# Loading and scaling a layer's residual 512 columns at a time within its output projection, in a two-layer decoder trunk

## The chip, the cores and the metric

The kernel runs on one core of one Trainium2 chip. The metric is the device time of one execution in microseconds (us), median of several runs. The engines are PE (TensorE: matmuls and transposes), DVE (VectorE), ACT (ScalarE), POOL (GpSimd) and SP (SyncE, which here issues transfers only). SP and POOL each have a DMA queue from which they issue transfers in program order. On-chip data lies in SBUF, 128 partitions wide; matmuls write PSUM, eight banks here, of which the kernel uses four for projections (`pjb`) and four for the rest (`mxb`).

## The reference

Two layers over 256 tokens of 2048 columns, all in float32: layer 0 mixes the tokens by a gated linear recurrence, layer 1 by a sparse attention. Each ends with an output projection, a residual and a layer norm:

```python
D_MODEL, SEQ, DEPTH = 2048, 256, 2
DEEPNORM_ALPHA = (2 * DEPTH) ** 0.25
def _layer_norm(x, g, b):
    mu = jnp.mean(x, -1, keepdims=True)
    xc = x - mu
    var = jnp.mean(xc * xc, -1, keepdims=True)
    return xc * lax.rsqrt(var + LN_EPS) * g + b
h = x
for i in range(DEPTH):
    y = _hgrn2_mixer(h, ...) if i == 0 else _nsa_mixer(h, ...)   # ends with (o * silu(z)) @ w_out
    h = _layer_norm(DEEPNORM_ALPHA * h + y, ln_g, ln_b)
```

For layer 1, `h` in `ALPHA * h` is the output of layer 0's norm, that is its normalized rows times `l0_ln_g` plus `l0_ln_b`. Applying these two to the normalized rows is the work that the change moves.

## The kernel before

The two tiles (`NT = 2`) of 128 tokens each are worked on through a list of projections with a weight matrix. Weights come in pieces of 256 rows by 512 columns (512 KB), loaded by `load` (L105) from SP's queue into a few slots named `wr`. So that one-pass products carry float32, each piece is split into a high part `wh` (ACT, L78) and a low part `wl` (DVE, L79), and the activations likewise (`bh` and `bl` for the input of layer 1's output projection, `ah` and `al` before). `tok_step` makes three matmuls for each tile and each 128 rows: high by high (L140), high by the weights' low (L141), low by high (L142). A piece of the output projection is 12 matmuls of 512 columns.

Layer 1's attention has four head groups: `query(g)` projects the queries (L185 to L188 and their kin), then `scores` makes the probabilities `p` (maximum, exponentials on ACT at L729 and L732, sums, L734 to L737 for the factors, L746 for the scaling of `p` on DVE), and `values` transposes `p` on PE (L762) and multiplies by the values, with a last copy on ACT (L774). `gate(g)` then multiplies by a gate (`zT`, ACT L786; DVE L789). Groups 2 and 3 are queried first and gated behind; so the last stretch of attention holds the scores and values of group 3 and the gate projections of groups 2 and 3, and PE's order there mixes the first pieces of the output projection among them.

The output projection of layer 1 has four column blocks `c` of 512 columns, each of 8 pieces. Blocks 0 to 2 go through `project`, block 3 through `project_by_tile`. Behind each block, `residual` adds `ALPHA * xr` to the product on DVE (L831) into `hb`, and takes the statistics (L833); behind the last block the norm follows and the output is stored (L854).

The residual itself: layer 0 leaves its normalized rows, before gain and bias, in a DRAM tile `norm0`. Behind the attention's code stands a loop over the four column blocks. It loads 512 columns of `norm0` for both tiles into `xr` (512 KB, L804), the gain and the bias of these columns, each broadcast to 128 partitions, into `gb` (256 KB each, L807), all from POOL's queue, and on POOL multiplies (L809) and adds (L810) for each tile. `xr` and `gb` take the slots of layer 1's multiplied input (`ah`, `al`), which are free after its last gate projection has read them. The pool `n1` with `hb` comes to be where attention's buffers were. The rows `l1_ln_g` and `l1_ln_b` of the last norm (1 MB each) are loaded by `row` (L820) from SP's queue, behind block 1 in the code.

The order of each engine's instructions isn't that of the code. `tile.TileContext(nc, schedule_with_timeline_sim=True)` orders them by a simulated timeline, data dependences, buffers and priorities; `parts` raises the priority of the weight splits. The engines then run their lists in order and wait for each other by semaphores.

Of the kernel before, what the change touches and what calls it, by code (L numbers as in the profile page):

```python
# [17 lines left out]
D = 2048  # L18
# [11 lines left out]
# the compressed blocks in the order that the kernel has them  # L30
# [5 lines left out]
# 500000 ** (-arange(0, 32, 2) / 32) in float32  # L36
# [5 lines left out]
# 2 pi in parts whose products with a small integer are exact  # L42
# [4 lines left out]
# The pairs of tokens in the order that the kernel has them: the second tile's are reversed.  # L47
PAIRS = list(range(64)) + list(range(127, 63, -1))
# column of each segment of l1_w_in
# [5 lines left out]
def trunk(ctx, tc, a, out):  # L55
# [20 lines left out]
    def split(hi, lo, src):  # L76
        """src = hi + lo, exactly, each of which the single pass products carry."""
        act.activation(hi, src, AF.Copy)  # L78
        dve.tensor_tensor(lo, src, hi.bitcast(F32), op=OP.subtract)  # L79

# [7 lines left out]
    class Pair:  # L88
        """Transposed activations, split: KG pairs of [128, 4, S]."""
# [12 lines left out]
    def load(w, j, c0, n):  # L102
        """Rows 256j .. 256j+255 of columns c0 .. c0+n-1."""
        raw = slot([128, 2, n], F32, "wr", 3, 1)
        nc.sync.dma_start(raw, w[256 * j:256 * (j + 1), c0:c0 + n].rearrange("(k p) n -> p k n", p=128))  # L105
        return raw
# [4 lines left out]
    # While there is room, a second pool holds a part of the slots.  # L111
# [13 lines left out]
    def slot(shape, dtype, name, n, more):  # L125
        """A tile of the n slots of a name, or of the n + more while there is room."""
# [17 lines left out]
    def project(xs, w, c0, also=None, n=512):  # L144
        """[tokens, n columns] of xs @ w, a bank for each tile of tokens."""
# [10 lines left out]
    def project_by_tile(xs, w, c0, after, behind=None, halve=False):  # L156
        """The same, one tile of tokens after the other, with after(t, bank) behind each. If that
        (or behind, for the first tile) names a matmul, the rest of the next tile's are queued after it."""
        ws = [weights(w, j, c0, 512) for j in range(KT // 2)]
        for t in range(NT):  # L160
            # the last one in two halves, where that is asked for
# [11 lines left out]
    def project_t(xs, w, c0, before=None):  # L173
        """[512 columns, tokens] of xs @ w: a bank for each two blocks of 128 columns."""
        ps = [pjb([128, 2, S]) for _ in range(2)]
        for j in range(KT // 2):
            hi, lo = before(j) if before else weights(w, j, c0, 512)
            for kk in range(2):
                k = 2 * j + kk
                xh, xl = xs.at(k, slice(0, S))  # L180
                for b in range(4):
                    o = ps[b // 2][:, b % 2]
                    c = slice(128 * b, 128 * (b + 1))
                    # one clearing of the bank serves both of its blocks
# [7 lines left out]
    def transposed(src):  # L192
        """[128 tokens, 4, 128] -> a bank of [128, 4, 128 tokens]."""
# [12 lines left out]
    # own[s, t]: s is t  # L206
    own = masks0.tile([128, 128], I32, name="own")
    # first[s, b]: s is the first of the b-th pair
    first = masks0.tile([128, 64], I32, name="first")
    # lvl[s, i, t, (b, j)]: s lies in the earlier half (the second one, in the second tile of tokens)  # L210
    # of the b-th block of 2m, m = 2 << i
    lvl = masks0.tile([128, 6, NT, 64], I32, name="lvl")
    # additive masks of the scores
# [12 lines left out]
    def columns(p, src):  # L226
        """A row of D values as a bank's [128, KT]."""
# [6 lines left out]
    def masks(p):  # L234
# [16 lines left out]
        # lower bounds of the forget gates: the softmax over one layer, less its first row  # L251
# [9 lines left out]
    def tables(p):  # L261
        dve.tensor_copy(g0c, columns(p, a["l0_ln_g"].rearrange("(k d) -> k d", d=128)))
        dve.tensor_copy(b0c, columns(p, a["l0_ln_b"].rearrange("(k d) -> k d", d=128)))
        # the tokens by partition and by column, and the last token of each compressed block
# [18 lines left out]
        # rotary tables  # L283
# [25 lines left out]
    w0 = a["l0_w_in"]  # L309

    # x, transposed, just ahead of the first projection's need of it
    xT = Pair("a")
    with tc.tile_pool(name="start", bufs=4) as start:
        # keeps the tensor engine's clock up until the first operands are there
# [37 lines left out]
    def recurrence(g, m0, ad, pf, pq):  # L352
        """The decayed scores of four heads, keys by queries: within a tile of tokens (into ad), and
        the first tile's keys with the second tile's queries. Built by doubling, with products of
        forget gates only, none of which exceeds one."""
# [14 lines left out]
        # within a pair of tokens: the products of each token's own query and key, and of the later  # L370
        # one's query with the earlier one's key, added up over the partitions
# [25 lines left out]
        for i in range(7):  # L397
# [10 lines left out]
            else:  # L408
                # The first tile's earlier halves and the second's, whose blocks are reversed, are
                # complementary: they are the keys of both tiles' later halves at once.  # L410
# [82 lines left out]
    def moments(p, hb, stats, t):  # L493
        """Mean and 1 / deviation of a row, from its chunks' statistics."""
# [42 lines left out]
    # Four blocks of 64 keys are what the top four select, and no key is further than the window:  # L537
    # both attend to every earlier key.
# [5 lines left out]
    def three(o, a, b, start, stop):  # L544
        """o += a @ b, of split operands."""
# [4 lines left out]
    def rotary(p, t, ps):  # L550
        """Out of the bank, and the first 32 of each head rotated."""
# [11 lines left out]
    class Compression:  # L563
        """The blocks of 32 keys or values, every 16 tokens, through the two layers of their MLP."""
# [4 lines left out]
        def flatten(self, src):  # L569
            """src: [128, 4, S] -> [d, place in the block, group, block], split."""  # L570
# [9 lines left out]
            # chunks of 16 tokens, in which the second tile's pairs are in reverse  # L580
            c = src.rearrange("p g (c l) -> p l g c", l=16)
            for i in range(2):
                fl = self.p.tile([128, 16, 4, NB], F32, name="fl")
                # (places among the blocks, the chunk of the first of them)
# [11 lines left out]
        def step(self, i):  # L596
            """The i-th eighth of the first layer."""
# [203 lines left out]
    for c in range(4):  # L801
# [4 lines left out]
        for i, name in enumerate(("l0_ln_g", "l0_ln_b")):  # L806
            nc.gpsimd.dma_start(gb[:, i], a[name][None, cs].to_broadcast([128, 512]))  # L807
# [90 lines left out]
```

## Time and profile before

| what | value |
|---|---|
| median of 3 runs | 1029.81 us |
| the three runs | 1028.95, 1029.81, 1035.2 us |
| span of the profiled execution | 1024.8 us |
| median of the runs less that span | 5.0 us |
| PE busy | 1000.4 us, 98% of the span |
| DVE, ACT, POOL busy | 66%, 53%, 14% |
| moved by DMA | 185.25 MB, 181 GB/s |

The profiled execution's own time is known as its span, from the first to the last instruction that the profiler recorded; the 5.0 us between it and the median lie around the span. Busy shares are of the span. Matmuls are pipelined, so that the duration of one overlaps that of the next: the pace is read from starts, not from durations.

### The profile page before, as it was taken

The numbers are of one execution on the slowest core, as the hardware profiler recorded it, in microseconds if no ns is written. First come the engines' busy times: TensorE is split into PE (matmuls) and PEld (weight loads), VectorE is DVE, ScalarE is ACT, GpSimd is POOL, SyncE is SP. The second block draws the span as 40 slices with busy tenths as digits, with TensorE's granted clock in tenths as the row PEclk, the third lists the DMA queues.
The fourth block names the chain that finished last, engine by engine and source line by source line (L and its number), as shares of the span: only waits on it lengthen the run. The fifth ranks groups of instructions, "written<-read, shape, count | busy, mean of one in ns | idle before, by whom it ended". The sixth has DMA issues, their size and how long they took to land.

```text
span 1024.8 us, 15936 instructions
## 1 busy us (share of the span) xinstructions
PE 1000.4 (98%) x6041; PEld 883.5 (86%) x6041; DVE 680.9 (66%) x1095; ACT 543.5 (53%) x864; POOL 148.5 (14%) x234
## 2 busy tenths in 40 slices
PE   9999999999999999999999999999999999979995
PEld 8988998899889988878889777989889889967885
DVE  6796568656865686656555566556857667885666
ACT  6654445444544454433575455455748666764431
POOL 0400300030003000310016310101020021180003
PEclk9999999999999999999999999999999999998998
DMA  8765465555555554457555677575453555564752
GB/s 293 259 219 164 155 185 165 165 157 183 164 165 160 183 163 164 165 192 248 174 192 171 202 236 232 149 231 180 144 149 119 154 156 155 164 215 149 262 164 82
DMA packets 99756, 185.25 MB, mean 181 GB/s; under 512 B 6096, under 2 KB 20512, under 8 KB 99168
## 3 DMA queue, kind: packets, MB, share of 16 engines
q1 hardware_dynamic: 96992, 174.48, 53.4%
q0 software_dynamic: 2688, 9.76, 3.2%
q8 instruction: 47, 0.77, 0.3%
q14 instruction: 29, 0.24, 0.1%
HBM read 180.02 MB, written 4.19 MB: 180 GB/s over the span
## 4 chain that ended last, share of the span: by engine, by line
PE 89%; DVE 4%; DMA 3%; ACT 2%; POOL 1%; issue 1%; SPq 0%; ACTq 0%; DVEq 0%
PE pjb L141 17%; PE pjb L142 17%; PE pjb L140 17%; PE pjb L185 9%; PE pjb L187 9%; PE pjb L188 9%; PE mxb L423 2%; DMA wr<-in_l_w_in_dram 1%; POOL fl L590 1%; PE mxb L196 1%; DVE wl L79 1%; PE mxb L546 1%; ACT wh L78 1%; PE mxb L547 1%; PE mxb L548 1%; PE mxb L762 1%
## 5 line engine op out<-in xcount | busy, mean ns | idle before, releaser
L79 DVE TENSOR_TENSOR wl<-wr,wh 128x1024 fp32r<-128x1024 f32 (+2 forms) x330 | 397.6, 1209 | 218.6 <-ACT wh L78 215.5
L78 ACT ACTIVATE wh<-wr 128x1024 fp32r<-128x1024 f32 (+2 forms) x330 | 340.3, 1036 | 334.6 <-PE pjb L142 150.8
L185 PE MATMUL pjb<-ah,wh 128*128 128x256 f32 x832 | 235.4, 284 | 0.7 <-ACT wh L78 0.7
L187 PE MATMUL pjb<-al,wh 128*128 128x256 f32 x832 | 235.4, 284 | 0.0
L188 PE MATMUL pjb<-ah,wl 128*128 128x256 f32 x832 | 234.3, 283 | 0.5 <-DVE wl L79 0.5
L141 PE MATMUL pjb<-wl,ah 128*128 128x512 f32 (+1 forms) x576 | 223.0, 387 | 2.5 <-DVE wl L79 2.4
L142 PE MATMUL pjb<-wh,al 128*128 128x512 f32 (+1 forms) x576 | 222.0, 386 | 0.0
L140 PE MATMUL pjb<-wh,ah 128*128 128x512 f32 (+1 forms) x576 | 221.0, 387 | 0.8 <-ACT wh L78 0.6
L185 PEld LDWEIGHTS pjb<-ah,wh 128*128 128x128 f32 x832 | 156.8, 189 | 1.7 <-ACT wh L78 1.1
L188 PEld LDWEIGHTS pjb<-ah,wl 128*128 128x128 f32 x832 | 156.2, 189 | 1.4 <-DVE wl L79 1.3
L187 PEld LDWEIGHTS pjb<-al,wh 128*128 128x128 f32 x832 | 156.1, 188 | 0.5
L141 PEld LDWEIGHTS pjb<-wl,ah 128*128 128x128 f32 x576 | 108.5, 188 | 26.6 <-DVE wl L79 5.2
L140 PEld LDWEIGHTS pjb<-wh,ah 128*128 128x128 f32 x576 | 108.0, 188 | 23.2 <-ACT wh L78 1.7
L142 PEld LDWEIGHTS pjb<-wh,al 128*128 128x128 f32 x576 | 108.5, 188 | 22.0
L141 PE MATMUL pjb<-wl,bh 128*128 128x512 f32 (+1 forms) x272 | 105.4, 387 | 0.0
L142 PE MATMUL pjb<-wh,bl 128*128 128x512 f32 (+1 forms) x272 | 105.0, 386 | 0.0
L140 PE MATMUL pjb<-wh,bh 128*128 128x512 f32 (+1 forms) x272 | 104.9, 386 | 0.0
L142 PEld LDWEIGHTS pjb<-wh,bl 128*128 128x128 f32 x272 | 51.8, 190 | 11.0 <-issue 0.2
L141 PEld LDWEIGHTS pjb<-wl,bh 128*128 128x128 f32 x272 | 51.8, 190 | 10.9
L140 PEld LDWEIGHTS pjb<-wh,bh 128*128 128x128 f32 x272 | 51.6, 190 | 10.9
L486 POOL TENSOR_TENSOR gz<-gz,gn 128x512 f32<-128x512 f32 x8 | 13.5, 1692 | 316.1 <-ACT gz L485 315.5
L557 POOL TENSOR_TENSOR rot<-qr,cc 128x128 f32<-128x128 f32 x14 | 9.5, 678 | 252.4 <-ACT qr L553 252.0
(223 smaller groups left out, 1054.0 us busy)
## 6 DMA issues: line engine op xcount, KB each, us to landing
wr<-in_l_w_in_dram SPq DMA_DIRECT2D x230, 512.0 KB, 3.6
wr<-in_l_w_out_dram SPq DMA_DIRECT2D x64, 512.0 KB, 4.3
wr<-in_l_w_in_dram SPq DMA_DIRECT2D x16, 280.0 KB, 2.9
wr<-in_l_cmp_w_k_dram SPq DMA_DIRECT2D x8, 512.0 KB, 4.1
wr<-in_l_cmp_w_v_dram SPq DMA_DIRECT2D x8, 512.0 KB, 4.2
xr<-in_x_dram POOLq DMA_DIRECT2D x4, 512.0 KB, 5.3
norm<-hb POOLq DMA_DIRECT2D x2, 1024.0 KB, 5.5
xr<-norm POOLq DMA_DIRECT2D x4, 512.0 KB, 6.8
```

What stands on the lines that cost most here:

```text
L78: act.activation(hi, src, AF.Copy)
L79: dve.tensor_tensor(lo, src, hi.bitcast(F32), op=OP.subtract)
L140: pe.matmul(ps, xh, wh, start=(k == 0), stop=False)
L141: pe.matmul(ps, xh, wl, start=False, stop=False)
L142: pe.matmul(ps, xl, wh, start=False, stop=(k == KT - 1))
L185: pe.matmul(o, hi[:, kk, c], xh, start=(k == 0 and b % 2 == 0), stop=False, skip_group_check=True)
L187: pe.matmul(o, hi[:, kk, c], xl, start=False, stop=False, skip_group_check=True)
L188: pe.matmul(o, lo[:, kk, c], xh, start=False, stop=(k == KT - 1), skip_group_check=True)
L196: last[0] = pe.transpose(ps[:, i], src[:, i], ident).ins
L423: pe.matmul(ps[:, h], km[:, h].rearrange("p b r j -> p (b r j)"), later, start=True, stop=True)
L486: pool.tensor_tensor(z, z, gn, op=OP.mult)
L546: pe.matmul(o, a[0], b[0], start=start, stop=False)
```

## The change

The loop behind attention goes. `fetch(c)` does the same for one block: it loads `xr` and `gb` from SP's queue, the weights' own, and multiplies and adds on POOL. It is called within the projection of its block: `project` gets a function `behind`, which it calls behind each piece's matmuls, and which fetches at the fourth piece (`j == 3`); the fetch of block 3 stands behind block 2. `xr` and `gb` now lie in the pool `n1`, `xr` in two buffers, `gb` in one. The diff, without lines in which only comments went:

```diff
@@ behind gate(3, os3)
-    # the residual of layer 1, in the slots of the activations that have been multiplied
-    xs = []
-    for c in range(4):
-        cs = slice(512 * c, 512 * (c + 1))
-        xr = acts.tile([128, NT, 512], F32, name="xr", tag="ah")
-        nc.gpsimd.dma_start(xr, norm0[:, cs].rearrange("(t p) d -> p t d", p=128))
-        gb = acts.tile([128, 2, 512], F32, name="gb", tag="al")
-        for i, name in enumerate(("l0_ln_g", "l0_ln_b")):
-            nc.gpsimd.dma_start(gb[:, i], a[name][None, cs].to_broadcast([128, 512]))
-        for t in range(NT):
-            pool.tensor_tensor(xr[:, t], xr[:, t], gb[:, 0], op=OP.mult)
-            pool.tensor_tensor(xr[:, t], xr[:, t], gb[:, 1], op=OP.add)
-        xs.append(xr)
...
+    def fetch(c):
+        cs = slice(512 * c, 512 * (c + 1))
+        xr = n1.tile([128, NT, 512], F32, name="xr")
+        nc.sync.dma_start(xr, norm0[:, cs].rearrange("(t p) d -> p t d", p=128))
+        gb = n1.tile([128, 2, 512], F32, name="gb", bufs=1)
+        for i, name in enumerate(("l0_ln_g", "l0_ln_b")):
+            nc.sync.dma_start(gb[:, i], a[name][None, cs].to_broadcast([128, 512]))
+        for t in range(NT):
+            pool.tensor_tensor(xr[:, t], xr[:, t], gb[:, 0], op=OP.mult)
+            pool.tensor_tensor(xr[:, t], xr[:, t], gb[:, 1], op=OP.add)
+        return xr
...
     for c in range(4):
         cs = slice(512 * c, 512 * (c + 1))
-        def residual(t, ps, c=c, xr=xs[c], parts=range(2)):
+        xr = []
+
+        def behind(j, c=c, xr=xr):
+            if j == 3:
+                xr.append(fetch(c))
+
+        def residual(t, ps, c=c, xr=xr, parts=range(2)):
+            xr = xr[0]
...
         if c < 3:
-            for t, ps in enumerate(project(oT, a["l1_w_out"], 512 * c)):
+            for t, ps in enumerate(project(oT, a["l1_w_out"], 512 * c, behind)):
                 residual(t, ps)
+            if c == 2:
+                last_xr = fetch(3)
             if c == 1:
                 widen()
                 g1, b1 = row("l1_ln_g"), row("l1_ln_b")
         else:
+            xr.append(last_xr)
             project_by_tile(oT, a["l1_w_out"], 512 * c, finish, halve=True)
```

SP's queue in the output projection, before; L105 loads a weight piece, L820 the rows of the last norm, L854 stores the output:

```order
L105 DMA wr<-in_l_w_out_dram 128x2x512 x15
L820 DMA l_ln_g<-in_l_ln_g_dram 128x2048
L820 DMA l_ln_b<-in_l_ln_b_dram 128x2048
L105 DMA wr<-in_l_w_out_dram 128x2x512 x17
L854 DMA out_dram<-hb 128x512 x8
```

And in the changed kernel, where L808 loads `xr`, L811 gain and bias, L819 the rows of the last norm:

```order
L105 DMA wr<-in_l_w_out_dram 128x2x512 x15
L808 DMA xr<-norm_72 128x2x512
L811 DMA gb<-in_l_ln_g_dram 128x512
L811 DMA gb<-in_l_ln_b_dram 128x512
L808 DMA xr<-norm_72 128x2x512
L819 DMA l_ln_g<-in_l_ln_g_dram 128x2048
L819 DMA l_ln_b<-in_l_ln_b_dram 128x2048
L105 DMA wr<-in_l_w_out_dram 128x2x512 x3
L811 DMA gb<-in_l_ln_g_dram 128x512
L811 DMA gb<-in_l_ln_b_dram 128x512
L808 DMA xr<-norm_72 128x2x512
L105 DMA wr<-in_l_w_out_dram 128x2x512 x3
```

The four residual loads and the eight of gain and bias stand among the pieces now; ahead of the piece numbered 14 (one of the 15 before it is a later piece, 19, which has a slot of its own) stand `xr` and `gb` of block 0 and `xr` of block 1 beside the two rows that stood there before.

DVE's order behind the last gate, before; `bl` is the low part of the projection's input, `wl` that of a piece, L831 the residual addition, L833 the statistics:

```order
L79 TENSOR_TENSOR bl<-o,bh 128x4x128 x2
L79 TENSOR_TENSOR wl<-wr,wh 128x1024 x3
L831 SCALAR_TENSOR_TENSOR hb<-xr,pjb 128x256 x2
L833 BN_STATS stats<-hb 128x6
L831 SCALAR_TENSOR_TENSOR hb<-xr,pjb 128x256 x2
L833 BN_STATS stats<-hb 128x6 x3
L79 TENSOR_TENSOR wl<-wr,wh 128x1024 x6
L831 SCALAR_TENSOR_TENSOR hb<-xr,pjb 128x256 x2
```

And in the changed kernel, where L837 is the residual addition and L839 the statistics:

```order
L79 TENSOR_TENSOR bl<-o,bh 128x4x128 x2
L79 TENSOR_TENSOR wl<-wr,wh 128x1024 x3
L837 SCALAR_TENSOR_TENSOR hb<-xr,pjb 128x256 x2
L839 BN_STATS stats<-hb 128x6 x2
L837 SCALAR_TENSOR_TENSOR hb<-xr,pjb 128x256 x2
L839 BN_STATS stats<-hb 128x6 x2
L79 TENSOR_TENSOR wl<-wr,wh 128x1024 x3
L837 SCALAR_TENSOR_TENSOR hb<-xr,pjb 128x256 x2
L839 BN_STATS stats<-hb 128x6 x2
L79 TENSOR_TENSOR wl<-wr,wh 128x1024
```

The residual addition of block 0 stands in the same place, ahead of the splits of pieces 14 to 16; that of block 1 stands three splits further up than before, ahead of pieces 17 to 19. On PE, ACT and DVE nothing ahead of these rows is ordered otherwise.

## Rows read from the trace of the kernel before

**Rows 1.** The page's head: busy us, share of the span and instructions.

```profile
PE 1000.4 (98%) x6041; PEld 883.5 (86%) x6041; DVE 680.9 (66%) x1095; ACT 543.5 (53%) x864; POOL 148.5 (14%) x234
```

**Rows 2.** Windows: stretch, us, busy (instructions) per engine, granted clock, DMA share, GB/s.

```profile
914.60:924.40 9.80, 2.33 (x9) 1.13 (x8) 7.98 (x9) 4.83 (x13) 9.50 (x8) 0.74 0.32 123
924.40:929.60 5.20, 5.16 (x15) 4.14 (x16) 4.68 (x7) 2.04 (x3) 0.00 (x0) 0.51 0.38 125
```

**Rows 3.** PE's timeline: start us, us, line, operation, out<-in.

```profile
914.24 0.39 PE L140 MATMUL pjb<-wh,bh 128*128 128x512 f32 x1
917.36 0.40 PE L142 MATMUL pjb<-wh,bl 128*128 128x512 f32 x1
929.80 0.39 PE L140 MATMUL pjb<-wh,bh 128*128 128x512 f32 x1
963.20 0.40 PE L141 MATMUL pjb<-wl,bh 128*128 128x512 f32 x1
971.64 0.39 PE L141 MATMUL pjb<-wl,bh 128*128 128x512 f32 x1
```

**Rows 4.** PE's groups, 914.7 to 929.75: busy us, mean ns, idle before, releasers.

```profile
L762 PE MATMUL mxb<-ident,p 128*128 128x128 f32 x8 | 2.5, 411 | 7.5 <-DVE p L746 5.3 <-ACT o L774 2.2
```

**Rows 5.** The chain of waits, 903 to 925: start us, us, what.

```profile
904.03 7.17 DMA wr<-in_l_w_out_dram
911.29 1.06 ACT wh L78
912.36 1.28 ACT L729
916.35 1.01 DVE st L734
922.90 1.49 DVE p L746
```

**Rows 6.** Landing of L105's loads, 880 to 1000; DMA issues (KB, us).

```profile
DMA to landing us min/median/max: 3.5/4.9/7.4
l_ln_g<-in_l_ln_g_dram SPq DMA_DIRECT2D x1, 1024.0 KB, 4.6
```

**Rows 7.** The tile gb: an operation that reads it, ns min/median/max.

```profile
L809 POOL TENSOR_TENSOR xr<-xr,gb x8: 1265/1298/1900, 893.8 to 919.7; 128x512 f32<-128x512 f32 x8
```

**Rows 8.** DVE's groups: first two 890 to 926, last two 600 to 890.

```profile
L734 DVE TENSOR_SCALAR st<-st 128x6 f32<-128x6 f32 x3 | 2.5, 817 | 2.6 <-ACT p L732 2.6
L746 DVE TENSOR_TENSOR p<-p,st 128x256 f32<-128x256 f32 x10 | 6.8, 738 | 0.0
L734 DVE TENSOR_SCALAR st<-st 128x6 f32<-128x6 f32 x13 | 2.2, 170 | 14.8 <-ACT p L732 14.7
L746 DVE TENSOR_TENSOR p<-p,st 128x256 f32<-128x256 f32 x38 | 13.8, 418 | 0.0
```

**Rows 9.** Timeline of ACT and POOL.

```profile
905.57 0.60 ACT L786 ACTIVATE zT<-pjb 128x512 f32<-128x512 f32 x1
916.06 2.51 POOL L810 TENSOR_TENSOR xr<-xr,gb 128x512 f32<-128x512 f32 x2
```

**Rows 10.** Timeline of SP's queue, DVE, ACT; last the idle time, its releaser.

```profile
946.63 0.34 SPq L820 DMA_DIRECT2D l_ln_g<-in_l_ln_g_dram  x1
954.08 0.75 DVE L831 SCALAR_TENSOR_TENSOR hb<-xr,pjb 128x256 f32<-128x256 f32 x2 [2.66 <-PE pjb L142]
955.74 1.07 DVE L833 BATCH_NORM_STATS2 stats<-hb 128x6 f32<-128x256 f32 x3
956.12 1.06 ACT L78 ACTIVATE wh<-wr 128x1024 fp32r<-128x1024 f32 x1 [5.96 <-DMA wr<-in_l_w_out_dram]
957.22 3.93 DVE L79 TENSOR_TENSOR wl<-wr,wh 128x1024 fp32r<-128x1024 f32 x3 [0.41 <-ACT wh L78]
957.49 1.06 ACT L78 ACTIVATE wh<-wr 128x1024 fp32r<-128x1024 f32 x1 [0.31 <-DMA wr<-in_l_w_out_dram]
```

**Rows 11.** Windows, columns as in rows 2.

```profile
946.00:991.00 45.00, 45.00 (x194) 36.18 (x193) 29.84 (x37) 21.00 (x20) 0.00 (x0) 1.00 0.73 246
```

## Prediction

> **What bounds the kernel now.** I read the page's head first, then the windows around the one stretch in which TensorE (PE) is not busy, then PE's rows in it, then the chain that leads there. The head has PE busy for 98% of the span [rows 1], so only two things can shorten the kernel: a gap in PE's row, or a stretch with its clock down. Both stand in one place. From 914.6 to 924.4 us PE is busy 2.33 of 9.80 us, and in the 5.20 us behind that the granted clock is 0.51, which is the lower level, 1.2 GHz [rows 2]. The gaps, 7.5 us, are all ahead of L762, the transposes of the attention probabilities of the last head group [rows 4]. The waiting costs twice.
>
> The loss is counted in instructions. From the matmul at 914.24 to the one at 929.80 [rows 3] lie 15.56 us, and PE has 24 instructions there (9 and 15 in the two windows [rows 2]), of which eight are transposes [rows 4]. At full clock a matmul of 512 columns takes 0.235 us: three weight pieces of 12 lie between 963.20 and 971.64 [rows 3]. A transpose is shorter; I give it 0.15. That is 16 x 0.235 + 8 x 0.15 = 5.0 us of work, so **10.6 us are lost** here.
>
> Why does PE wait? The chain of waits [rows 5], read backwards, goes through VectorE's (DVE's) scaling of the probabilities (L746 at 922.90), the small factors (L734 at 916.35), ScalarE's (ACT's) table load at 912.36 and the exponentials behind it, and the split of the fifth output weight piece at 911.29, behind which those stand in ACT's order. That piece was issued at 904.03, when DVE had freed its buffer, and took 7.17 us to land; the shortest landing of such a piece is 3.5, the median 4.9 [rows 6].
> Slow DVE steps and slow landing have one neighbour: here GpSimd (POOL) runs the 16 residual operations (L809, L810), 1.27 to 1.9 us each, the median 1.30 [rows 7], and its queue loads the residual. From 600 to 890 us L734 takes 170 ns and L746 418; from 890 to 926 their means are 817 and 738 [rows 8]. L734 at 916.35 lies inside the two POOL operations that run from 916.06 [rows 9], and lasts 1.01 us.
>
> **What the change removes.** The POOL operations and the twelve POOL loads leave this stretch; PE, DVE and ACT keep their order in it. I redo the chain with undisturbed durations. By rows 8, L734 and L746 lose 3 x 0.65 + 10 x 0.32 = 5.1 us to POOL; about half of these executions come ahead of 904.03, so the fifth piece is issued 2.5 us earlier, near 901.5. With 3.5 to 4.9 us to land it is in at 905.0 to 906.4. ACT cannot take it before its zT step (905.57 + 0.60 [rows 9]), which waits for PE. Then follow the split, 1.06, to 907.4; the table load, 1.28, to 908.7; the exponentials, 2.7 (913.64 to 916.35), to 911.4; on DVE, L734 0.17, four steps of L746's shape or smaller at 0.2 to 0.42, and four L746 in 1.7: 914.1 to 915.0. In before the last L746 of the chain ends at 924.4. PE runs out of other work at 914.6, so 0 to 0.4 us of the wait stay. I take none: **all 10.6 us go**. If the landing takes 7 us again, 2 to 3 us stay.
>
> **What it adds.** The same POOL operations, and the loads (four of 512 KB, eight of 256 KB, 4.2 MB) now stand in SP's queue within the output projection. SP has room: an issue takes 0.34 us [rows 10], so twelve take some 4, in a stretch where it mostly waits for buffers. What counts is what stands behind them. (Times here are those of before; in the new kernel all of them come 10.6 earlier.)
> First, the residual of columns 0 to 511 needs the attention's buffers free, as the row l1_ln_g does now, at 946.63 [rows 10]. It goes ahead of that row and of weight piece 14 (counted from 0) with 1.5 MB. Pieces that queue behind each other reach ACT 1.37 us per 512 KB apart (956.12, 957.49) [rows 10], so 1.5 MB are 4.1 us. Piece 14 then reaches ACT at 960.2, its low half is done 1.1 + 1.3 later (the split of 1.06 on ACT, and a third of the three in 3.93 on DVE), at 962.6, and PE wants that at 963.20 [rows 3, 10]. **Margin 0.6 us**, where it was 4.7. Piece 15 is wanted 2.8 us later and comes 1.4 later, so it is safer.
> Second, in DVE's order the residual addition of block 0 (L837) stands ahead of the splits of pieces 14 to 16, and it waits for POOL. A load of 1 MB takes 4.6 us to land [rows 6], so POOL starts near 951.3, and four operations of 1.27 to 1.9 us end at 956.4 to 958.9. With 2.7 us for the addition and its statistics (954.08 to 956.81 [rows 10]) DVE is free by 961.6 at worst. Piece 14's split waits for that from 961.3: 0.3 at worst, within its margin.
> Third, gain and bias have one buffer, so the next pair is issued when POOL is done with block 0, at 956.4 to 958.9, behind pieces 14 to 16, which land until 962.9, and is in at 964.3. POOL's third operation of block 1, the last for the first tile, ends at 968.1 to 970.0. The addition and statistics of that tile take 1.4 us and the split of piece 17 behind them 1.3: 970.8 to 972.7, and up to 1.3 later if POOL's fourth operation holds it up. PE wants it at 971.64 [rows 3]: between 0.8 us of margin and 2.4 of stall. Pieces 18 and 19 stand the same way with 2.8 us more each, and later pieces with more.
> I take **1.0 us of stall** for this part, nearer to the lower end because POOL's median is 1.30. A stall of that size does not bring the clock down: behind the first wait the matmul at 917.36 still takes 0.40 [rows 3]. Ahead of the last head group nothing moves, and behind the last matmul the same instructions stand in the same order.
>
> A rule speaks against the change. The Trainium skill, "SBUF — State Buffer", section "Who interferes with whom", says that a DVE instruction with two inputs in SBUF and a GpSimd instruction that reads SBUF shut each other out for the whole instruction. By that rule the weight splits, which read wr and wh, would be held up by the moved operations as L746 is now, by up to 16 x 1.3 = 21 us of DVE time, and the sum would be rival (a)'s. The trace agrees in kind: L746, with two inputs in SBUF, goes from 418 to 738 ns. Whether DVE has room for it is seen without the rule: from 946 to 991 it is busy 29.8 of 45 us [rows 11].
>
> **The rivals.** (a) *The wait moves along.* For it: from 946 to 991 the DMA engines are busy 0.73 of the time at 246 GB/s [rows 11]; 4.2 MB more are 93 GB/s, 339 in all, and 246/0.73 is 337, so the queue would be full. At 246 GB/s the 1.5 MB ahead of piece 14 take 6.4 us instead of 4.1, and it stalls 1.7 us; piece 17 stalls 2.4; and 2.5 (half of 5.2) are paid for the clock if the gaps add up. Against it: queued pieces come at 383 GB/s (512 KB in 1.37 us). Price 6.6 us instead of 1: 1025.8. (b) *A part of the wait stays*, with the fifth piece late or ACT late for another reason: 2 to 3 us more than forecast: 1022.7. (c) *POOL is not the cause*, and DVE's small steps are slow at the end of attention for another reason: nothing is gained, 1.0 lost: 1030.8. Against it stand the 13 and 38 earlier executions in rows 8. (d) *Slower*: one buffer for gain and bias ties the blocks into a chain of load, POOL, addition and splits. At its longest that is 7.4 (the longest landing [rows 6]) + 4 x 1.9 + 2.7 + 3 x 1.3 = 21.6 us, and PE needs 96 x 0.235 = 22.6 for a block. Beyond that, each of the three blocks with a fetch stalls for some 3.6 us (half of the 7.5 at which the clock fell) and pays 2.5 for the clock: 18.3 - 10.6 = 7.7 us slower, 1037.5. It decides only if landing and POOL are at their longest every time.
>
> **How the numbers follow.** The profiled execution's span is 1024.8 us and the median of the three runs 1029.8, so 5.0 lie around the span. 1024.8 - 10.6 + 1.0 = 1015.2, and with the 5.0 **1020.2 us**. About 1% is what a measurement of this kernel can tell from no change; that line is at 1019.5, and without any stall the time would be 1019.2, just across it. My case holds 60% (1018.2 to 1021.6, the lower end if a transpose costs less than 0.15), and in nearly six tenths of it the stall is small enough for that line. (a) has 19%, (b) 11%, (c) 5%, (d) 5%. All of these four lie within 1%, except the far end of (d) and the part of (b) that is paid back by a smaller stall later. The range of 8 in 10 takes in my case, (b) and most of (a): 1017.8 to 1026. Faster by over 1% 0.38, within 1% 0.59, slower by over 1% 0.03.
>
> **What would show it.** From 880 us to the end of attention POOL's row is empty, L734 and L746 have their 0.17 and 0.42 us again, the fifth output piece lands in under 5 us, and PE has neither a gap at L762 nor a clock of 0.51. In the output projection PE's gaps, if any, stand at the first matmul that reads a low half (L141), released by DVE, and DVE's waits name POOL. I am wrong if L762 still waits, if the gaps in the projection exceed 3 us in sum, or if the clock drops there.

## The result, and the profile after

The changed kernel takes **1021.19 us** (median of 4 runs, 1020.80 to 1022.54) against 1029.87 before (4 runs, 1028.95 to 1035.20): ratio 0.9913, 95% interval 0.9891 to 0.9935, 0.9% faster, so within 1%. The prediction was 1020.2. The profiled execution has a span of 1019.8 us, 5.0 less than before.

The head of the page after answers to [rows 1], its windows over the last attention group to [rows 2] and over the projection to [rows 11]:

```profile
PE 999.9 (98%) x6041; PEld 883.4 (87%) x6041; DVE 669.6 (66%) x1095; ACT 543.3 (53%) x864; POOL 143.1 (14%) x222
```

```profile
905.00:915.00 10.00, 10.00 (x60) 8.70 (x59) 6.33 (x15) 9.21 (x20) 0.00 (x0) 1.00 0.57 192
915.00:925.00 10.00, 10.00 (x53) 8.24 (x52) 6.34 (x8) 4.95 (x7) 0.00 (x0) 1.00 0.47 157
946.00:991.00 45.00, 44.07 (x185) 34.03 (x183) 27.75 (x36) 16.87 (x16) 20.97 (x14) 1.00 0.84 290
```

From 905 to 925 us PE is busy throughout at full clock, where before it was busy 2.33 of 9.80 us and then ran 5.20 us at 0.51. POOL is idle there, as it should be. In the projection PE now loses 0.93 of 45 us, which it did not before, POOL is busy for 21, and the transfers run at 290 GB/s instead of 246. DVE's small steps, for which [rows 8] stand before (its groups from 880 to 926 us):

```profile
L746 DVE TENSOR_TENSOR p<-p,st 128x256 f32<-128x256 f32 x12 | 4.4, 417 | 0.0
...
L734 DVE TENSOR_SCALAR st<-st 128x6 f32<-128x6 f32 x4 | 0.7, 167 | 5.4 <-ACT p L732 5.4
```

They are back at 417 and 167 ns. The fifth output piece, next, in SP's queue and on ACT (answering to [rows 5]); the first of these two rows joins three issues:

```profile
903.14 5.20 SPq L105 DMA_DIRECT2D wr<-in_l_w_out_dram  x3
...
907.70 1.06 ACT L78 ACTIVATE wh<-wr 128x1024 fp32r<-128x1024 f32 x1
```

It was issued at 903.14, and its split began 4.56 us later; before, 7.26.

**How much, and where.** PE's instructions can be paired between the two traces by counting the output projection's matmuls from the last. The partner of the L140 at 914.24 in [rows 3] is the L140 at 915.96, that of the one at 929.80 is at 920.45; the last one starts at 1013.47 before and at 1008.21 after. Three rows of PE's timeline after at which it waits stand with them:

```profile
915.96 0.39 PE L140 MATMUL pjb<-wh,bh 128*128 128x512 f32 x1
...
920.45 0.39 PE L140 MATMUL pjb<-wh,bh 128*128 128x512 f32 x1
...
955.21 0.50 PE L141 MATMUL pjb<-wl,bh 128*128 128x512 f32 x1 [0.52 <-DVE wl L79]
...
991.49 0.50 PE L141 MATMUL pjb<-wl,bh 128*128 128x512 f32 x1 [0.59 <-DVE wl L79]
...
993.60 0.61 PE L140 MATMUL pjb<-wh,bh 128*128 128x512 f32 x2 [0.67 <-ACT wh L78]
```

So the stretch of 15.56 us is now 4.49: **11.1 us gained**. The kernel after is 1.7 us behind at its start (915.96 to 914.24), 9.35 ahead at its end, and only 5.26 ahead at the last matmul: **4.1 us given back** in the projection. The 1.7 arises far ahead of the change, where both kernels run the same instructions and PE waits for weights: from 600 to 605 us the granted clock was 0.66 in the execution profiled after and 1.00 in the one before. It isn't the change's. PE's groups from 930 to 1010 us say who ends the waits:

```profile
L141 PE MATMUL pjb<-wl,bh 128*128 128x512 f32 (+1 forms) x120 | 44.4, 370 | 1.4 <-DVE wl L79 1.3
...
L140 PE MATMUL pjb<-wh,bh 128*128 128x512 f32 (+1 forms) x120 | 42.8, 367 | 0.8 <-ACT wh L78 0.8
```

Idle time there is 2.2 us; from start to start it is more, since a matmul behind a wait doesn't overlap one ahead of it (990.50 to 991.49 is 0.99 us for a pace of 0.235). In the control run, below, 2.5 are given back instead of 4.1.

### The profile page after: what moved, and what is told of

Its sections match the earlier page's. It is cut to its first block, busy times and chain, and to the rows that moved or that the text cites. A ratio compares the mean times of both kernels' runs of the same rounds, so it can differ in the third digit from the quotient of the medians.

```text
span 1019.8 us, 15942 instructions
## 1 busy us (share of the span) xinstructions
PE 999.9 (98%) x6041; PEld 883.4 (87%) x6041; DVE 669.6 (66%) x1095; ACT 543.3 (53%) x864; POOL 143.1 (14%) x222
## 4 chain that ended last, share of the span: by engine, by line
PE 84%; DMA 7%; DVE 3%; POOL 2%; ACT 2%; issue 1%; SPq 0%; ACTq 0%; DVEq 0%; POOLq 0%
PE pjb L141 15%; PE pjb L142 15%; PE pjb L140 15%; PE pjb L185 10%; PE pjb L187 10%; PE pjb L188 10%; DMA wr<-in_l_w_in_dram 3%; PE mxb L423 2%; DVE wl L79 2%; DMA wr<-in_l_w_out_dram 2%; ACT wh L78 1%; DMA gb<-in_l_ln_g_dram 1%; PE mxb L196 1%; POOL fl L590 1%; PE mxb L546 1%; PE mxb L548 1%
## 5 line engine op out<-in xcount | busy, mean ns | idle before, releaser
L140 PE MATMUL pjb<-wh,ah 128*128 128x512 f32 (+1 forms) x576 | 221.4, 387 | 1.1 <-ACT wh L78 1.1
L140 PEld LDWEIGHTS pjb<-wh,ah 128*128 128x128 f32 x576 | 108.5, 189 | 23.6 <-ACT wh L78 1.8
L140 PE MATMUL pjb<-wh,bh 128*128 128x512 f32 (+1 forms) x272 | 103.1, 384 | 0.8 <-ACT wh L78 0.8
L140 PEld LDWEIGHTS pjb<-wh,bh 128*128 128x128 f32 x272 | 51.1, 188 | 12.3 <-ACT wh L78 1.7
```

Source lines behind the costliest of these rows:

```text
L140: pe.matmul(ps, xh, wh, start=(k == 0), stop=False)
```

## The experiments

Two theories for the gain. **A**: GpSimd's operations hold up DVE's steps in the last attention group. **B**: the residual's transfers make the fifth piece land late. For what is given back: **P**, the residual stands ahead of pieces in SP's queue; **Q**, its bytes take bandwidth, whatever the queue; **O**, GpSimd's operations make the splits of weights longer. Each time is a median, and its ratio is to runs of the kernel before on the same chip (1027.41 us in the first four experiments, 1028.38 in the next four, 1027.60 in the last four). Between kernels that differ by 1 to 2 us the intervals of these ratios overlap; there the traces decide, not the times.

**The control**, the changed kernel once more.

> The changed kernel once more, as the control for the runs beside it. Expected 1021 us, 8 to 9 below the kernel before. Theory A (GpSimd's two-input operations slow VectorE's small steps in the last attention group, and the moved work costs a few us in the projection) and theory B (the residual's transfers, not the operations, make the fifth output weight piece late, and with it the last group) say the same here.

1020.87 us, ratio 0.9931 (0.9914 to 0.9948). The other times are read against this one.

**GpSimd's operations without the transfers.** Behind the last gate of the changed kernel:

```diff
+    for c in range(4):
+        dr = acts.tile([128, NT, 512], F32, name="dr", tag="ah")
+        dg = acts.tile([128, 2, 512], F32, name="dg", tag="al")
+        pool.memset(dr, 1.0)
+        pool.memset(dg, 1.0)
+        nc.gpsimd.dma_start(dr[:, :, 0:8], norm0[:, 512 * c:512 * c + 8]...)
+        for t in range(NT):
+            pool.tensor_tensor(dr[:, t], dr[:, t], dg[:, 0], op=OP.mult)
+            pool.tensor_tensor(dr[:, t], dr[:, t], dg[:, 1], op=OP.add)
```

> The changed kernel, with 16 GpSimd operations of the removed shape (128x512, two inputs) put back behind the last gate on scratch tiles in the old slots, whose contents come from memsets and from 8-column transfers; no order changes on PE, VectorE, ScalarE and SP. Theory A: L734 takes 0.6 us or more and L746 0.6 or more again while they run, PE waits at L762 for 3 to 8 us with a drop of the clock behind it, and the time is 1025 to 1031. They start some us earlier than in the kernel before, since no 512 KB transfer holds them up, so the loss may be smaller than 10.6. Theory B: without the transfers nothing is lost, L762 does not wait, 1020 to 1022.

1031.95 us, ratio 1.0043 (1.0028 to 1.0058): the whole gain is gone, and more. DVE's groups from 880 to 930 us, then a row of its timeline and three of POOL's, and PE's groups from 905 to 935:

```profile
L79 DVE TENSOR_TENSOR wl<-wr,wh 128x1024 fp32r<-128x1024 f32 x10 | 21.7, 2179 | 1.5 <-ACT wh L78 1.5
L746 DVE TENSOR_TENSOR p<-p,st 128x256 f32<-128x256 f32 x12 | 6.5, 715 | 0.0
...
L734 DVE TENSOR_SCALAR st<-st 128x6 f32<-128x6 f32 x4 | 1.2, 300 | 3.0 <-ACT p L732 3.0
```

```profile
913.47 8.66 DVE L79 TENSOR_TENSOR wl<-wr,wh 128x1024 fp32r<-128x1024 f32 x1
...
913.59 2.51 POOL L807 TENSOR_TENSOR dr<-dr,dg 128x512 f32<-128x512 f32 x2
916.05 2.52 POOL L806 TENSOR_TENSOR dr<-dr,dg 128x512 f32<-128x512 f32 x2
918.53 2.52 POOL L807 TENSOR_TENSOR dr<-dr,dg 128x512 f32<-128x512 f32 x2
```

```profile
L141 PE MATMUL pjb<-wl,bh 128*128 128x512 f32 x18 | 8.3, 462 | 0.9 <-DVE wl L79 0.9
...
L762 PE MATMUL mxb<-ident,p 128*128 128x128 f32 x16 | 3.6, 348 | 2.3 <-ACT o L774 2.3
...
L547 PE MATMUL mxb<-pt,vals 128*128 128x512 f32 x2 | 1.1, 564 | 2.9 <-DVE pt L79 2.9
```

L746 takes 715 ns again and a split 2.18 us in the mean. One split, alone 1.22 us, took 8.66: it began with a run of six POOL operations that follow each other without a pause (913.59 to 921.05) and ended 1.1 us behind them. PE's waits come behind these. They don't all stand where they stood before: L762 waits 2.3 us here, against 7.5, and the steps behind it more; and the run has eight memsets that the kernel before lacks. Theory A holds as the main cause, and B falls as that: there were no transfers to speak of.

**Memsets in their place.** The three lines from `for t` on become

```diff
+        for i in range(6):
+            pool.memset(dr, float(i))
```

> As the run with the 16 operations, but in their place 24 GpSimd memsets of 128x1024 (0.96 us each in the trace of the kernel before), about the same time on GpSimd, which only write SBUF. Theory A in its narrow form (what holds VectorE up is that both engines read SBUF with two inputs): L734 0.17, L746 0.42, no wait at L762, 1020 to 1022. Rival: any GpSimd work at this place holds VectorE up; then as the run with the operations, 1025 to 1031. Theory B: 1020 to 1022.

1029.32 us, ratio 1.0016 (1.0000 to 1.0032), 8.5 us over the control: the narrow form of A is wrong in its time. Its rows (views as above):

```profile
L746 DVE TENSOR_TENSOR p<-p,st 128x256 f32<-128x256 f32 x12 | 4.4, 431 | 0.0
...
L734 DVE TENSOR_SCALAR st<-st 128x6 f32<-128x6 f32 x4 | 3.8, 961 | 5.3 <-ACT p L732 5.3
```

```profile
907.64 1.22 DVE L79 TENSOR_TENSOR wl<-wr,wh 128x1024 fp32r<-128x1024 f32 x1
908.77 9.66 DVE L727 TENSOR_SCALAR st<-st 128x6 f32<-128x6 f32 x1
...
905.81 12.59 POOL L806 MEMSET dr<- 128x1024 f32 x14 [0.49 <-DMA dr<-norm]
```

```profile
L762 PE MATMUL mxb<-ident,p 128*128 128x128 f32 x16 | 3.4, 349 | 6.3 <-ACT o L774 6.3
```

The steps with two inputs in SBUF aren't held up: L746 takes 431 ns, and the split at 907.64, in the middle of the memsets, 1.22 us. But the steps with one input and scalars are: L734 takes 961 ns in the mean, and L727, a step of 6 columns, 9.66 us, up to the end of the fourteen memsets in a row (and two splits that began behind it ended with it, at 918.43). So both kinds of GpSimd work hold DVE up, each other steps. The Trainium skill, "SBUF — State Buffer", section "Who interferes with whom", has this distinction: two inputs in SBUF against a GpSimd instruction that reads, `tensor_scalar` in a two-port mode against GpSimd. The trace agrees with it in both halves (431 ns and 961 ns); that L734 and L727 ran in such a mode isn't shown by it.

**The transfers without the operations.** The kernel before, whose GpSimd operations write into `hb`, which exists only behind attention:

```diff
-        for t in range(NT):
-            pool.tensor_tensor(xr[:, t], xr[:, t], gb[:, 0], op=OP.mult)
-            pool.tensor_tensor(xr[:, t], xr[:, t], gb[:, 1], op=OP.add)
-        xs.append(xr)
+        xs.append((xr, gb))
...
+        for t in range(NT):
+            pool.tensor_tensor(hb[:, t, cs], xr[:, t], gb[:, 0], op=OP.mult)
+            pool.tensor_tensor(hb[:, t, cs], hb[:, t, cs], gb[:, 1], op=OP.add)
...
-                dve.scalar_tensor_tensor(h, xr[:, t, 256 * u:256 * (u + 1)], ALPHA, ps[:, n * i:n * (i + 1)],
+                dve.scalar_tensor_tensor(h, h, ALPHA, ps[:, n * i:n * (i + 1)],
```

> The kernel before with its twelve residual transfers where they were (GpSimd's queue, behind the last gate, slots of the multiplied activations), but the 16 GpSimd operations write into hb, which exists only once attention's buffers are free, so they run within the output projection; the residual addition reads hb. PE, ScalarE and SP keep the order of the kernel before. Theory A: L734 and L746 at 0.17 and 0.42 us, no wait at L762 and no drop of the clock there; the output projection is not short of transfers, so nothing is given back: 1018 to 1020, 1 to 3 below the changed kernel. Theory B: the transfers still delay the fifth piece to 7 us of landing, L762 waits 4 us or more, 1025 to 1030.

1019.55 us, ratio 0.9921 (0.9902 to 0.9939). DVE's groups from 880 to 930, PE's from 905 to 935:

```profile
L746 DVE TENSOR_TENSOR p<-p,st 128x256 f32<-128x256 f32 x12 | 4.3, 416 | 0.0
...
L734 DVE TENSOR_SCALAR st<-st 128x6 f32<-128x6 f32 x4 | 0.7, 168 | 5.4 <-ACT p L732 5.4
```

```profile
L762 PE MATMUL mxb<-ident,p 128*128 128x128 f32 x16 | 2.8, 284 | 1.6 <-ACT o L774 1.6
```

With all transfers in their old place the steps are short, and 1.6 us of wait remain, without a drop of the clock. That much is left to B. PE has no wait in the projection, though the splits are longer there (from 946 to 1000 us, this run, then the changed kernel):

```profile
L79 DVE TENSOR_TENSOR wl<-wr,wh 128x1024 fp32r<-128x1024 f32 x19 | 28.7, 1526 | 9.9 <-ACT wh L78 9.8
...
L79 DVE TENSOR_TENSOR wl<-wr,wh 128x1024 fp32r<-128x1024 f32 x18 | 24.2, 1356 | 15.1 <-ACT wh L78 14.6
```

So long splits alone, O as it stands, don't make PE wait.

**The transfers in GpSimd's queue**, within the projection: `nc.sync.dma_start` becomes `nc.gpsimd.dma_start` three times in `fetch`.

> The changed kernel with its twelve residual transfers issued from GpSimd's queue instead of SP's, at the same place in the projection. The question is what makes PE wait there (2.3 to 3.8 us in the two traces of the changed kernel, at pieces 14, 25, 29 and 30). Theory P, the place in SP's queue: piece 14 no longer stands behind 1.5 MB, PE's waits in the projection fall below 0.7 us, and the time is 1017.5 to 1019.5. Theory Q, the transfers' bandwidth whatever their queue: 1.5 to 4 us of waits stay, 1020 to 1022. Theory O, GpSimd's operations make the weight splits (L79) longer there: as Q.

1022.29 us, ratio 0.9940 (0.9919 to 0.9961): not better than the control. The wait at piece 14 is gone, as P says, but the pieces now land later (median 7.6 us from 940 to 1000, against 6.7 in the changed kernel), and PE waits at piece 17 and twice from 987 us on, with a clock of 0.70 from 991 to 995 us. PE's groups from 930 to 1010:

```profile
L141 PE MATMUL pjb<-wl,bh 128*128 128x512 f32 (+1 forms) x119 | 44.2, 372 | 2.4 <-DVE wl L79 2.4
...
L140 PE MATMUL pjb<-wh,bh 128*128 128x512 f32 (+1 forms) x119 | 43.4, 372 | 1.0 <-ACT wh L78 1.0
```

**GpSimd's operations cut to 8 columns**, `xr[:, t, 0:8]` and `gb[:, i, 0:8]` in `fetch`.

> The changed kernel with the 16 GpSimd operations cut to 8 columns each, so that most of the residual is neither scaled nor shifted; the transfers stay as they are. Theory O: the splits L79 take 1.22 us throughout and PE's waits in the projection fall below 1 us: 1018 to 1019.5. Theories P and Q: piece 14 still lands some 11 us after its issue and PE waits for it some 1 us; 1019.5 to 1021.5.

1019.60 us, ratio 0.9912 (0.9891 to 0.9933). DVE's splits from 946 to 1000 us, and PE's groups from 946 to 975:

```profile
L79 DVE TENSOR_TENSOR wl<-wr,wh 128x1024 fp32r<-128x1024 f32 x18 | 21.8, 1222 | 18.1 <-ACT wh L78 17.6
```

```profile
L141 PE MATMUL pjb<-wl,bh 128*128 128x512 f32 x40 | 16.1, 402 | 0.9 <-DVE wl L79 0.9
```

A split takes 1.22 us (1.36 in the changed kernel), and PE has no wait from 975 to 1000, where the changed kernel has 1.6. That at piece 14 stays (1.0 from start to start), and 0.4 of idle time at piece 18 is new. So P is right for piece 14, and the late waits come from the length of POOL's operations. That need not be through the splits: SP's waits, from 935 to 995 us, first in the changed kernel and then here, show a second way:

```profile
SPq L811 <- POOL xr L814: 11.4, 3, 5.4
...
SPq L811 <- POOL xr L814: 1.7, 3, 0.8
```

SP waited 11.4 us, in three waits, the longest 5.4, until POOL had freed the one buffer of gain and bias, and the pieces behind in its queue waited with it; here it waited 1.7.

**The rows of the last norm in GpSimd's queue.**

```diff
-        nc.sync.dma_start(r, a[name][None, :].to_broadcast([128, D]))
+        nc.gpsimd.dma_start(r, a[name][None, :].to_broadcast([128, D]))
```

> The changed kernel with the two rows of the last norm (1 MB each) issued from GpSimd's queue; they run at about the same time, but piece 14 has 2 MB less ahead of it in SP's queue. PE, VectorE and ScalarE keep the changed kernel's order. Theory P: piece 14 lands 3 to 5 us after its place in the queue comes and its wait of 1.2 us is gone; 1019 to 1020.5. Theory Q: the rows still take their share of the bandwidth, the wait at piece 14 stays above 0.6; 1020 to 1022.

The call of `row` also moves in the code, from behind block 1 to ahead of block 3; the two rows are issued at 938.03 and 938.60 us, about when they were (939.19 and 939.70).

1019.40 us, ratio 0.9914 (0.9893 to 0.9934). PE has no wait from 946 to 975 us, so that at piece 14 is gone; from 975 to 1000 it still waits 1.7.

**Half of the transfers early.** As the run with all transfers early, but only `range(2)` there; blocks 2 and 3 are loaded into `n1` from GpSimd's queue.

> A mixture, to see whether it beats both kernels: the transfers of blocks 0 and 1 early in GpSimd's queue, into the slots of the multiplied activations, those of blocks 2 and 3 in GpSimd's queue once attention's buffers are free, all 16 GpSimd operations into hb within the projection. In the run with all transfers early PE still waited 1.8 us at L762 and nowhere in the projection. Theory A with P: half of the early transfers, so the wait at L762 is below 1 us, and none in the projection: 1017 to 1019. Theory Q: the 2.1 MB in the projection cost 1 to 2 us of waits: 1019 to 1020.5.

1029.93 us, ratio 0.9984 (0.9949 to 1.0019), and of its 12 executions three took 1017.4 to 1017.9, one 1024.1, eight 1029.0 to 1032.1. Neither theory said that. In the profiled one (DVE, POOL, then PE's groups from 930 to 1010):

```profile
939.07 22.59 DVE L79 TENSOR_TENSOR wl<-wr,wh 128x1024 fp32r<-128x1024 f32 x2 [0.18 <-ACT wh L78]
...
939.66 5.04 POOL L834 TENSOR_TENSOR hb<-xr,gb 128x512 f32<-128x512 f32 x4
...
955.75 3.69 POOL L835 TENSOR_TENSOR hb<-hb,gb 128x512 f32<-128x512 f32 x3
```

```profile
L141 PE MATMUL pjb<-wl,bh 128*128 128x512 f32 (+1 forms) x101 | 39.5, 391 | 11.2 <-DVE wl L79 11.2
```

The first row joins two splits. Together they take 22.59 us instead of 2.5, that is some 20 of waiting, through a run of all 16 POOL operations from 939.66 to 959.44 without a pause. This is theory **S**: what counts is how long POOL runs on without one.

**The same with pauses.**

```diff
         for t in range(NT):
+            nc.gpsimd.dma_start(gb[:, 0, 0:8], a["l0_ln_g"][None, 512 * c:512 * c + 8].to_broadcast([128, 8]))
             pool.tensor_tensor(hb[:, t, cs], xr[:, t], gb[:, 0], op=OP.mult)
```

> The mixture with half of the transfers early was slow (1029.9) in most executions and fast (1017.4 to 1017.9) in some; in the profiled one a weight split on VectorE, L79, took 20 us and ended when GpSimd's run of 16 operations ended. Here each multiplication is preceded by an 8-column transfer into its operand, so that the same GpSimd operations come in short runs with pauses of some 2 us between. Theory S: a VectorE step with two inputs in SBUF can be kept out for the whole of an unbroken run of GpSimd operations, so pauses bound the wait: no split above 4 us, no wait of PE above 1 us in the projection, 1017 to 1019 in every execution. Rival: the sum of GpSimd's time is what counts, or the transfers; then 1025 to 1030 again.

1020.56 us, ratio 0.9927 (0.9914 to 0.9940), all executions between 1018.9 and 1021.4. The longest split:

```profile
941.74 5.89 DVE L79 TENSOR_TENSOR wl<-wr,wh 128x1024 fp32r<-128x1024 f32 x1 [0.18 <-ACT wh L78]
...
942.31 2.55 POOL L835 TENSOR_TENSOR hb<-xr,gb 128x512 f32<-128x512 f32 x2
944.81 1.30 POOL L836 TENSOR_TENSOR hb<-hb,gb 128x512 f32<-128x512 f32 x1
946.05 0.58 POOL L834 DMA_DIRECT2D gb<-in_l_ln_g_dram  x1
```

It takes 5.89 us and ends 1.0 behind 946.64, where POOL has issued a transfer instead of an operation. S fits: with the same operations and large transfers the long executions are gone. But it isn't separated from the place of the operations, which the small transfers also move later: POOL stands idle for 5.85 us up to 955.70. The bound of 4 us that was expected is missed, and 1.5 us of waits stay in PE's row.

**The same on VectorE**: `dve.tensor_tensor` for both operations of the mixture.

> The same mixture with the 16 operations on VectorE instead of GpSimd, some 16 x 0.65 = 10 us more of VectorE's time in the projection, where it was busy 30 of 45 us. Theory S: no operation of GpSimd is left there, no split above 1.3 us: 1016.5 to 1018.5, the fastest of all. Rival: VectorE's list becomes the bound, the splits come late and PE waits 2 us or more: 1020 to 1023.

1020.40 us, ratio 0.9924 (0.9910 to 0.9938): in the rival's range. No split is long, but PE waits at piece 14 (1.7 us of idle time), since DVE's list has operations that wait for transfers ahead of the split. The execution in the trace is the shortest of the six (1017.31 us); what the others lost isn't known.

**On VectorE in the changed kernel, with the rows in GpSimd's queue, and without that.** Both operations in `fetch` become `dve.tensor_tensor`; the first kernel moves the rows as above too.

> The changed kernel with the two rows of the last norm in GpSimd's queue and the 16 operations on VectorE. By the runs so far the first takes away the wait at piece 14 (theory P), the second those at pieces 25 to 30 (theory O): PE's waits in the projection fall below 0.7 us, 1017.5 to 1019. Rival: VectorE's own 10 us more take the place of what GpSimd cost, 1019.5 to 1022.

> The changed kernel with the 16 operations on VectorE instead of GpSimd, the rows and the residual's transfers as they are in SP's queue. Theory O with P: the wait at piece 14 stays (0.7 to 1.3 us), those at pieces 25 to 30 go: 1018.5 to 1020. Rival: VectorE becomes the bound, 1021 to 1024.

With the rows moved **1017.43 us** (1017.03 to 1018.17), ratio 0.9900 (0.9887 to 0.9913), without 1017.88, ratio 0.9903 (0.9889 to 0.9918). Both beat the kernel before. Their executions (1017.03 to 1019.23) also lie below all ten of the changed kernel (1019.93 to 1022.54), but those ran on other chips. On the control's the kernel before took nearly the same time (1027.41 and 1027.60 us), and the interval of its ratio (0.9914 to 0.9948) lies just clear of the first's and overlaps the second's. The first kernel's splits from 935 to 1000 us, and its window over the projection; then PE's groups of the second from 946 to 975 us:

```profile
L79 DVE TENSOR_TENSOR wl<-wr,wh 128x1024 fp32r<-128x1024 f32 x21 | 25.5, 1221 | 6.1 <-ACT wh L78 5.5
```

```profile
946.00:991.00 45.00, 45.00 (x195) 36.20 (x194) 39.17 (x58) 19.01 (x18) 0.00 (x0) 1.00 0.85 287
```

```profile
L141 PE MATMUL pjb<-wl,bh 128*128 128x512 f32 x40 | 16.0, 399 | 0.5 <-DVE wl L79 0.5
...
L140 PE MATMUL pjb<-wh,bh 128*128 128x512 f32 x39 | 14.4, 399 | 0.3 <-ACT wh L78 0.3
```

In the first PE is busy for all 45 us, with as many bytes in the projection (287 GB/s) as the changed kernel has: Q falls as a cause by itself, since the same traffic costs nothing once POOL's operations are gone and piece 14 has less ahead of it. In the second the wait at piece 14 stays and the late ones are gone.

## Why the prediction was right, and where not

**What the change removes: right, in place and size.** 10.6 us were said to go, 11.1 went; the half us is the transposes, put at 0.15 us each: in 4.49 us, 16 matmuls at 0.235 leave 0.09 for each of the eight. POOL's operations are the main cause: put back, with memsets in place of the transfers, they cost 11 us, and the transfers alone leave 1.6 of wait. The redone chain held: the issue near 901.5 was 903.14 - 1.7 = 901.4, and with a landing of 3.5 to 4.9 its split began 4.56 later.

**What it adds: the place partly right, the size wrong.** The step that failed is the 1.0 us of stall; 4.1 and 2.5 us were given back in the two traces. Of the 4.1, 1.2 are at piece 14, 0.1 at piece 17 and 2.8 from piece 25 on.
The first term, piece 14, was mis-sized. 1.5 MB were put at 4.1 us, by the pace of queued pieces. The timeline of SP's queue (three pieces joined) and of ACT after:

```profile
941.37 2.75 SPq L105 DMA_DIRECT2D wr<-in_l_w_out_dram  x3
...
952.84 1.06 ACT L78 ACTIVATE wh<-wr 128x1024 fp32r<-128x1024 f32 x1 [12.01 <-DMA wr<-in_l_w_out_dram]
```

The piece reaches ACT at 952.84. Before, that was 956.12, or 946.8 with the 9.35 taken off: 1.5 MB cost 6.1 us, near the 6.4 of rival (a), and the margin of 0.6 became a wait of some 1.2. The pace of queued pieces had not changed: the next two reach ACT at 954.18 and 955.56. What was slower were the residual's own loads: by issue and time to landing `xr` of block 0 is in at 941.96 and the 512 KB of gain and bias at 944.96, 3.0 us later, where 1.37 had been counted. Why they are slower no run shows. Moving two other megabytes out of the queue removed the wait at piece 14.
The second and third terms were right: the split of piece 17 ends just as PE wants it (a delay of 0.1 in the trace after), where 0.8 of margin to 2.4 of stall were given.
"Later pieces with more" margin was wrong, and it cost more than piece 14. The waits at 991.49 and 993.60 are at pieces 29 and 30. SP's queue and DVE's timeline after:

```profile
974.34 0.34 SPq L811 DMA_DIRECT2D gb<-in_l_ln_g_dram  x1
...
983.75 5.23 DVE L79 TENSOR_TENSOR wl<-wr,wh 128x1024 fp32r<-128x1024 f32 x4 [6.08 <-ACT wh L78]
```

The load of gain and bias of block 3 waits until 974.34 for POOL to free their one buffer (the 5.4 us of SP's waits above). Pieces 25 to 28, behind it in the queue, are issued from 975.25 on and reach ACT from 982.65 on. Their four splits take 5.23 us, no longer than undisturbed, and end 0.06 to 0.35 us before PE wants them; pieces 29 and 30 need the slots that the splits of 25 and 26 free, and are late. The working let the one buffer delay the addition of block 1, but not the pieces that stand behind the load in SP's queue. It also gave each later piece 2.8 us more, while in the last block PE works by tile and takes a piece every 1.4 us (six matmuls).
That POOL's operations lengthen the splits (1.36 us in the mean, 1.22 without them), which was weighed through the rule and left in rival (a), has a part too: in the control's trace the splits of pieces 25 to 28 take 6.20 us together. Cutting the operations short, or moving them to DVE, removed the late waits, but took away both delays at once, so how much each costs stays open.

**The rivals.** (a) was near for piece 14 in its 6.4 us, but not in its bandwidth: the changed kernel does move 290 GB/s, and the kernel on DVE 287 without any wait. The changed kernel paid nothing for the clock there. (b) didn't happen; (c) is refuted by the operations put back without the transfers; (d) didn't come at its price, but its chain of load, POOL and load through the one buffer is what SP's 11.4 us of waits show.

**The sum** came closer than its terms. From before to after the last matmul moves by +1.7 - 11.1 + 4.1 = -5.3 us, against -9.6 predicted. That the median still lies 1.0 from the forecast is luck in the base: 5.0 us were added for what lies around the span, but in the run that was profiled after, time and span differ by 1.7 (1021.53 and 1019.8). The profiled execution before was thus probably some 3 us faster than its median. Over all runs of the kernel before its times range from 1024.65 to 1035.20.

## What to carry to other kernels

Work on GpSimd isn't free because it is off the chain: look at the mean of VectorE's small steps in the stretches in which GpSimd runs and in those in which it doesn't, and count the difference for all of them, in the old place and in the new. What matters is which of VectorE's steps meet it and how long GpSimd runs without a pause; where VectorE has room, the same operations on VectorE itself cost less (1017.43 us, the best kernel here). A load that is moved into a queue is paid by the piece behind it, and not at the pace of the pieces (6.1 us here, where that pace gave 4.1). If it has to wait for a buffer that another engine frees, everything behind it in the queue waits too.

## What the hardware showed that was not expected

A VectorE step may wait far longer than one GpSimd operation. The Trainium skill, "SBUF — State Buffer", section "Who interferes with whom", says that whoever issues first gets the shared ports for the whole instruction, and the other is blocked. Here no GpSimd operation of this shape takes over 3.2 us (the longest, 966.40 to 969.58 in the changed kernel, itself meets splits), and yet one pair of splits lost some 20 us, a 6-column step 9.5 (9.66 for some 0.17), a split 7.4 (8.66 for 1.22), each up to the end of an unbroken run of GpSimd operations or to its first pause. It doesn't always happen: in the kernel before POOL runs from 913.21 to 924.10 without a pause, and no step of DVE in that time takes over 1.6 us (L746 at 922.90 1.49 [rows 5]); three of twelve executions of the mixture took no longer than the best kernels, though no trace of these was kept. What decides between the two wasn't settled.
